# RWKV units of a hybrid decoder layer: which queue issues the value and gate loads of a unit's end

## The chip, the cores and the metric

The kernel runs on one core of a Trainium2 chip. The metric is the device time of one execution in microseconds (us), as the median of repeated runs. A core has a tensor engine (PE in the profile; its weight loads are PEld), a vector engine (DVE), a scalar engine (ACT), GpSimd (POOL) and a sync engine (SP). Each takes its instructions in order and waits on semaphores for the others. DMA transfers are issued by SP, ACT or POOL and carried out by 16 DMA engines.

## The reference

One layer on 1024 tokens of 1024 features, all in float32. One projection gives the columns of an attention group and of an RWKV-7 group; the two group outputs are concatenated and projected, and a feed-forward block follows.

```python
z = _rms_norm(x, norm_mix_pre) @ w_in
attn = _rms_norm(_dilated_attention(q, k, v), attn_out_gain)
rw = _rwkv7(r_r, k_r, v_r, xw, xa, xg, ...)
x = x + _rms_norm(concat([attn, rw]) @ w_out, norm_mix_post)
x = x + _rms_norm(square(relu(_rms_norm(x, norm_ffn_pre) @ w_ffn_up)) @ w_ffn_down, norm_ffn_post)
```

The change is in the RWKV-7 group. Its state S of 64 x 64 for each of 8 heads runs over the tokens, and the end of a unit is the second part of this:

```python
S_t = S_{t-1} diag(w_t) - (S_{t-1} kk_t)(kk_t*a_t)^T + v_t k_t^T ;  y_t = S_t r_t
yn = (y - mean) * rsqrt(var + GN_EPS) * gn_w + gn_b     # per head
out = (yn + sum(r*k*r_k) * v) * g                       # v: values, g: gate
```

## The kernel before, in words

The 1024 tokens are cut into 8 units of 128 tokens, and a unit into two chunks of 64 (c_ = 0, 1). For the RWKV group the kernel first works on pairs of heads (norms, pre_pair, subst, merge), which leave their results in DRAM, and then on the units. A unit n consists of

- `unit_ab`: loads AR and K, multiplies them on PE (p<-AR,K) and masks the products on DVE into T (L593). PE's p uses two PSUM banks in turn, so the next p waits until L593 has read the last.
- `unit_e`: E on PE from Zp and TR, evacuated by ACT (L618).
- `unit_c`, the recurrence, for each chunk: PE multiplies HV (O<-HV), ACT copies a half to VU (L654), PE multiplies VU (O<-VU), DVE adds into HV (L660) and scales it into the HV of the next chunk (L661); ACT copies the result to Y (L662), once L660 has been done. The next chunk's O<-HV needs L661.
- `unit_g`, the unit's end: loads bv (the values, from v_d) and gg (the gate, from g_d), works out the group norm of Y (L681 and the small steps after it), scales and shifts bv (L684, L685), and ends with L688 (Y + bv) and L689 (Y times gg). Y is then stored to r_d (L691).

bv and gg have one buffer each. The loads for unit n wait until L688 and L689 of unit n-1 have read theirs. Until the units begin, the same buffers serve other tiles of pre_pair.

Between these steps PE works off the projections z_aq, z_ak and z_avB of the attention group, in pieces of 0.7 us. z_aq and z_ak are split into a high part by ACT (evh, L721) and a low part by DVE (evl, L722), and the low part is stored to qk_d by POOL (L724).

What sets the order: `drive` runs through the jobs with a table of waiting times (`WAIT`) and writes out PE's and SP's instructions in that order, under `tc.manual_schedule`. The order of DVE, ACT and POOL is chosen by the scheduler, from when it expects an instruction's inputs; POOL's DMAs are among these. All engines then run in the order that was written.

The functions that the diff touches, with the line numbers of the profile (`G` is POOL, `nc.sync` is SP, `t5` takes a tile of 128 x 512 from the pool of the units):

## Time and profile before

| | |
|---|---|
| median of 3 runs | 1283.39 us (1283.11 to 1285.42) |
| the profiled execution | 1283.58 us |
| its span on the core | 1281.8 us |
| busy PE, DVE, ACT, POOL | 98%, 70%, 49%, 3% of the span |
| granted TensorE clock | 0.997 |
| the units (bv's loads) | 290.3 to 421.9 us of the span |

Times in rows of the timeline count from the start of the span: start, duration, engine, line, operation, out<-in with buffer numbers left out, form, and in brackets the idle time of the engine just before and what ended it. In rows of waits the figures are total us, number of times, longest. In rows of a tile the durations are min/median/max in ns. In rows of windows each stretch has the busy time of PE, PEld, DVE, ACT and POOL with their instruction counts, then the granted clock, the DMA share and GB/s. "To landing" is the time from the start of a DMA's issue until its data is there.

### The profile page before, as it was taken

How to read it: one execution, taken by the hardware profiler on the slowest of the kernel's cores; microseconds unless marked ns; L12 is line 12 of the kernel's file. 1: busy time of each engine (PE TensorE's matmuls, PEld its weight loads, DVE VectorE, ACT ScalarE, POOL GpSimd, SP SyncE). 2: the span in 40 equal slices, each digit the busy share in tenths (PEclk: the TensorE clock that was granted, in tenths of full speed). 3: DMA queues.
4: the chain of work that ended last, by engine and by line, in shares of the span. 5: the costliest groups of instructions: out<-in, count | busy, mean ns of one | idle time of the engine just before them, and what ended most of it. 6: DMA issues, size and time to landing. Idle time of an engine off the chain costs nothing.

```text
span 1281.8 us, 24136 instructions
## 1 busy us (share of the span) xinstructions
PE 1251.9 (98%) x9648; PEld 1043.8 (81%) x9648; DVE 897.4 (70%) x1643; ACT 621.7 (49%) x1048; POOL 43.2 (3%) x61
## 2 busy tenths in 40 slices
PE   6989999999999999999999999999999999999997
PEld 5778888898789788888887888888887888888886
DVE  7867779533777668767789877677666875446884
ACT  8653433234544378766565444344433544443442
POOL 0000000000000000000000000000000001000221
PEclk9999999999999999999999999999999999999999
DMA  6445767968875766234243653444467983555642
GB/s 246 146 181 160 207 164 196 278 188 261 252 240 151 271 238 208 70 104 145 104 151 138 204 159 139 154 163 146 151 231 249 363 322 109 183 193 197 197 160 103
DMA packets 165312, 241.10 MB, mean 188 GB/s; under 512 B 56304, under 2 KB 91376, under 8 KB 165200
## 3 DMA queue, kind: packets, MB, share of 16 engines
q1 hardware_dynamic: 154672, 213.86, 51.7%
q10 hardware_dynamic: 9088, 20.98, 5.0%
q0 software_dynamic: 1440, 4.72, 1.0%
q8 instruction: 76, 1.25, 0.4%
q14 instruction: 36, 0.29, 0.1%
HBM read 162.16 MB, written 77.09 MB: 187 GB/s over the span
## 4 chain that ended last, share of the span: by engine, by line
PE 79%; DVE 10%; DMA 5%; ACT 4%; issue 2%; SPq 0%; DVEq 0%; ACTq 0%
PE dX L50 12%; PE X L50 10%; PE pm L50 7%; PE dZ L50 7%; PE Z L50 5%; PE z_v L50 4%; PE dY L50 3%; PE z_ak L50 3%; PE z_r L50 3%; PE Y L50 3%; PE po L50 2%; PE z_aq L50 2%; PE pT L952 2%; PE pS L50 2%; PE z_avA L50 2%
## 5 line engine op out<-in xcount | busy, mean ns | idle before, releaser
L50 PE MATMUL dX<-wow,wou 128*128 128x512 f32 x768 | 175.5, 390 | 0.5 <-DVE wow L1271 0.5
L50 PEld LDWEIGHTS dX<-wow,wou 128*128 128x128 f32 x768 | 143.9, 188 | 31.5 <-DVE wow L1271 1.3
L50 PE MATMUL dZ<-wow,wou 128*128 128x512 f32 x384 | 87.4, 389 | 0.0
L50 PEld LDWEIGHTS dZ<-wow,wou 128*128 128x128 f32 x384 | 72.1, 188 | 15.0
L1271 DVE TENSOR_TENSOR wou<-ur,wou 128x1024 fp32r<-128x1024 f32 x56 | 71.2, 1273 | 6.1 <-ACT wou L1270 5.6
L1270 ACT ACTIVATE wou<-ur 128x1024 fp32r<-128x1024 f32 x56 | 58.5, 1048 | 21.1 <-DMA ur<-u_d 13.8
L1270 ACT ACTIVATE wow<-wd 128x1024 fp32r<-128x1024 f32 x32 | 33.8, 1060 | 68.4 <-PE dX L50 24.5
L1271 DVE TENSOR_TENSOR wow<-TK,wow 128x1024 fp32r<-128x1024 f32 x24 | 30.6, 1274 | 50.0 <-ACT wow L1270 50.0
L1271 DVE TENSOR_TENSOR wow<-wd,wow 128x1024 fp32r<-128x1024 f32 x32 | 39.5, 1237 | 26.9 <-ACT wow L1270 26.5
L1368 ACT ACTIVATE r<-u 128x512 f32<-128x512 f32 x48 | 30.1, 626 | 54.5 <-DVE u L1366 54.4
L1270 ACT ACTIVATE wow<-TK 128x1024 fp32r<-128x1024 f32 x24 | 25.4, 1059 | 62.9 <-PE dX L50 32.5
L942 ACT ACTIVATE S<-S,mn 128x1024 f32<-128x1024 f32 (+7 forms) x64 | 49.2, 769 | 7.6 <-DVE mn L940 6.2
L50 PE MATMUL pm<-WO,mxr 128*128 128x512 f32 x192 | 49.1, 400 | 0.0
L1576 POOL TENSOR_TENSOR E<-E,gpF 128x512 f32<-128x512 f32 x12 | 22.4, 1881 | 755.3 <-DMA xf<-x_d 595.1
L940 DVE CUSTOM_DVE_ANT_0 S<-pS,stripT 128x512 f32<-128x512 f32 (+3 forms) x64 | 37.4, 589 | 13.6 <-PE pS L50 13.1
L50 PE MATMUL pm<-WO,mxa 128*128 128x512 f32 x192 | 46.1, 395 | 0.1
L50 PE MATMUL Z<-HB,wo 128*128 128x512 f32 x192 | 46.1, 389 | 0.0
L952 PE MATMUL pT<-cst,S 128*128 128x128 f32 x288 | 43.6, 277 | 2.4 <-ACT PT L954 1.4
L50 PE MATMUL z_aq<-hT,wh_aq 128*128 128x512 f32 x128 | 44.3, 404 | 0.0
L50 PE MATMUL z_ak<-hT,wh_ak 128*128 128x512 f32 x128 | 44.0, 402 | 0.0
L50 PE MATMUL z_k<-hT,wh_k 128*128 128x512 f32 x128 | 43.8, 400 | 0.0
L50 PE MATMUL dY<-wow,wou 128*128 128x512 f32 x192 | 43.7, 389 | 0.0
(399 smaller groups left out, 3097.1 us busy)
## 6 DMA issues: line engine op xcount, KB each, us to landing
ur<-u_d SPq DMA_DIRECT2D x56, 512.0 KB, 4.2
u_d<-S SPq DMA_DIRECT2D x64, 256.0 KB, 2.4
wd<-in_wdown_dram SPq DMA_DIRECT2D x32, 512.0 KB, 4.5
u_d<-u SPq DMA_DIRECT2D x48, 256.0 KB, 2.5
TK<-in_wdown_dram SPq DMA_DIRECT2D x24, 512.0 KB, 6.6
wr_upa<-in_wup_dram SPq DMA_DIRECT2D x16, 512.0 KB, 3.6
wr_upb<-in_wup_dram SPq DMA_DIRECT2D x16, 512.0 KB, 4.1
x<-in_x_dram SPq DMA_DIRECT2D x8, 512.0 KB, 6.9
```

Of the source, the lines that this page charges most:

```text
L50: return PE.matmul(o, lhsT, rhs, start=start, stop=stop, skip_group_check=True)
L940: V.tensor_tensor_reduce(Sx[:, lo:hi], pS[:, :hi - lo], stripT[:, so:so + hi - lo], 1.0, 3e38 if k == 0 else mn[:, 0:1], OP.add, OP.min, a ...
L942: at["exp"] = A.activation(Sx[:, :w], Sx[:, :w], AF.Exp, scale=-1.0, bias=mn[:, nbk - 1:nbk], accum_out=at[p, "den"][:, i, h:h + 1])
L952: PE.transpose(pt[:, j], Sx[:, (4 * k + j) * P:(4 * k + j + 1) * P], ident)
L1270: A.activation(w[:, 0, 0:n], raw, AF.Copy)
L1271: low = E.tensor_tensor(w[:, 1, 0:n], raw, w[:, 0, 0:n].bitcast(F32), OP.subtract)
L1368: A.activation(r, src, AF.Relu)
L1576: G.tensor_tensor(e, e, gn[n], OP.mult)
```

## The change

The two loads of `unit_g` are issued by POOL instead of SP, for all 8 units:

```diff
             bv, gg = t5(f"bv{n}", "bv"), t5(f"gg{n}", "gg")
-            nc.sync.dma_start(bv, v_d[ts, :])
-            nc.sync.dma_start(gg, g_d[ts, :])
+            G.dma_start(bv, v_d[ts, :])
+            G.dma_start(gg, g_d[ts, :])
```

PE's instructions keep their order. SP's list loses 16 DMAs and keeps the order of the rest. The loads take places on POOL that the scheduler chooses, and with them it moves the instructions of DVE that use them. In the rows, the number behind a name is a buffer's: bv_3960 is unit 1's, bv_4193 unit 2's, bv_4287 unit 3's, bv_4892 unit 5's, and Y_3875 and Y_4540 are the Y of units 1 and 4.

On POOL, the loads of units 1 to 3 among the stores of evl (+ is new):

```order
 L724 DMA qk_d<-evl_aq_0_3853 128x512
+L673 DMA bv_3960<-v_d 128x512
+L674 DMA gg_3961<-g_d 128x512
 L724 DMA qk_d<-evl_aq_1_4072 128x512
+L673 DMA bv_4193<-v_d 128x512
+L674 DMA gg_4194<-g_d 128x512
+L673 DMA bv_4287<-v_d 128x512
+L674 DMA gg_4288<-g_d 128x512
 L724 DMA qk_d<-evl_ak_0_4331 128x512
```

Each load stands on POOL as an instruction that waits for its buffer to come free, and the stores behind it wait with it.

On DVE, where unit 1's end and the recurrence of unit 2 (HV) meet the masks of unit 4 (T):

```order
 L689 TENSOR_TENSOR Y_3875<-Y_3875,gg_3961 128x512
 L660 TENSOR_TENSOR HV_3838<-O_1_4155,HV_3838 64x512
+L684 TENSOR_TENSOR bv_4193<-bv_4193,BON 128x512
 L661 TENSOR_TENSOR HV_4057<-HV_3838,PcL 64x512
 L593 TENSOR_TENSOR T_4_4222<-p_4_0_4223,cst 128x512
 L593 TENSOR_TENSOR T_4_4222<-p_4_0_4224,cst 128x512
```

The first step on unit 2's values has moved ahead of L661 and of two masks; it stood some twelve instructions later.

On DVE, where unit 4's end and the recurrence of unit 5 meet:

```order
 L688 TENSOR_TENSOR Y_4540<-Y_4540,bv_4653 128x512
 L689 TENSOR_TENSOR Y_4540<-Y_4540,gg_4654 128x512
+L684 TENSOR_TENSOR bv_4892<-bv_4892,BON 128x512
+L685 TENSOR_TENSOR bv_4892<-bv_4892,gw_3502 128x512
 L660 TENSOR_TENSOR HV_4507<-O_1_4831,HV_4507 64x512
 L661 TENSOR_TENSOR HV_4771<-HV_4507,PcL 64x512
```

Both steps on unit 5's values now stand ahead of L660 and L661 of that unit. Units 1 and 4 have moved in the same way as unit 5, unit 3 as unit 2 (L684 between L660 and L661 of its first chunk). L684 of unit 0 has moved up into the substitution of the last pair (L503, L505), behind the second of its products. Units 6 and 7 keep their places on DVE.

## Prediction

> **What bounds the kernel now.** I read the page first (span, busy shares), then the windows of busy time, then the waits of the tensor engine, and last the tile bv and the timeline around each of its eight loads.

> ```profile
> span 1281.8 us, 24136 instructions
> PE 1251.9 (98%) x9648; PEld 1043.8 (81%) x9648; DVE 897.4 (70%) x1643; ACT 621.7 (49%) x1048; POOL 43.2 (3%) x61
> 290.00:436.00 146.00, 141.43 (x1958) 121.30 (x1953) 99.13 (x228) 69.26 (x115) 5.40 (x10) 1.00 0.73 227
> 342.00:346.00 4.00, 3.31 (x87) 3.10 (x88) 3.75 (x7) 1.46 (x3) 0.00 (x0) 1.00 1.03 362
> 388.00:392.00 4.00, 4.00 (x68) 3.51 (x66) 3.90 (x9) 2.89 (x5) 0.00 (x0) 1.00 0.02 4
> ```

> PE is busy 98% of the span and runs in an order written out by hand, so its idle time is all that the kernel can gain, and any new PE idle time is lost for good. The unit ends lie between 290 and 436 us: PE works 141.43 of 146.00 us there, so 4.6 us is the most that the change can win. The last two figures of a row are the DMA share and GB/s: the DMA engines are full at 342 to 346 us and empty at 388 to 392.

> The loads that move, and what PE waits for in this stretch (total, times, longest):

> ```profile
> L673 SPq DMA_DIRECT2D bv<-v_d x8: 314/423/458, 290.3 to 421.9; - x8
> L684 DVE TENSOR_TENSOR bv<-bv,BON x8: 683/692/694, 295.2 to 424.5; 128x512 f32<-128x512 f32 x8
> L685 DVE TENSOR_TENSOR bv<-bv,gw x8: 691/692/694, 295.9 to 425.2; 128x512 f32<-128x512 f32 x8
>   DMA bv<-v_d: 8.3, 5
> DMA to landing us min/median/max: 2.6/4.3/7.7
> PE O L50 <- ACT VU L654: 1.9, 3, 0.7
> PE p L50 <- DVE T L593: 0.6, 1, 0.6
> PEld O L50 <- DMA VU<-vc_d: 0.4, 1, 0.4
> ```

> DVE stands still 8.3 us for bv, five times. PE waits for none of these loads and hardly for any load (0.4 us); it waits for DVE and ACT, in the recurrence O, HV, VU and in the masks T. So the question is not how long SP takes to issue, but which DVE work stands behind L684 while its load is under way.

> **The change part by part.** *SP loses 16 issues.* At 0.42 us each that is 6.8 us of a queue that PE waits for by 0.4 us at most. I take 0; the gain is 0 to 0.4 us.

> *POOL gains 16 issues*, at the price of its other DMAs:

> ```profile
> L724 POOL DMA_DIRECT2D qk_d<-evl_aq x8: 539/540/710, 230.4 to 442.4; - x8
> DMA to landing us min/median/max: 2.8/5.1/8.2
> ```

> 16 x 0.54 is 8.6 us on an engine that is busy 5.4 of these 146 us: 0. Queued behind the loads are the stores of evl. A load waits for its slot (bv is free after L688 of the unit before, gg after L689), and by the DVE order each evl behind it is computed after that, so a store loses at most two issues, 1.1 us, and its reader is the attention part much later: 0. What counts is the landing time of a 256 KB load from POOL, which the trace does not show. The nearest rows are POOL's stores of that size (2.8 to 8.2, median 5.1) and the same loads from SP (2.6 to 7.7). I take 5.1, and SP's own landing in units 4 and 5, where the engines are less loaded.

> *DVE's order moves.* In units 1 to 5 L684 now stands earlier, with the recurrence behind it. Unit 2, the row of PE last and SP's old issue ahead of it:

> ```profile
> 343.54 0.69 DVE L688 TENSOR_TENSOR Y<-Y,bv 128x512 f32<-128x512 f32 x1
> 345.04 0.68 DVE L660 TENSOR_TENSOR HV<-O,HV 64x512 f32<-64x512 f32 x1
> 345.76 0.68 DVE L661 TENSOR_TENSOR HV<-HV,PcL 64x512 f32<-64x512 f32 x1
> 346.37 0.68 DVE L593 TENSOR_TENSOR T<-p,cst 128x512 f32<-128x512 f32 x1
> 353.11 0.69 DVE L684 TENSOR_TENSOR bv<-bv,BON 128x512 f32<-128x512 f32 x1 [2.38 <-DMA bv<-v_d]
> 345.36 0.42 SPq L673 DMA_DIRECT2D bv<-v_d  x1
> 347.10 0.49 PE L50 MATMUL p<-AR,K 64*128 64x128 f32 x2 [0.59 <-DVE T L593]
> ```

> POOL can issue bv when L688 of unit 1 ends: 344.2 as before, or up to 1.4 earlier, since L684 and L685 of unit 1 leave the stretch ahead; half of it gives 343.5. Landing 348.6. L684 then starts 3.6 us after L660; L661 and L593 follow 0.6 and 0.7 us apart, so L593 starts at 349.9 instead of 346.37. PE's p matmul already waits for it, so PE loses all of it: **+3.5**. In the kernel before, L684 came after this L593 and its wait hit nobody.

> Unit 5, with SP's landing time of this load, and the ACT steps that follow L660:

> ```profile
> 391.52 0.69 DVE L688 TENSOR_TENSOR Y<-Y,bv 128x512 f32<-128x512 f32 x1
> 394.21 0.68 DVE L660 TENSOR_TENSOR HV<-O,HV 64x512 f32<-64x512 f32 x1 [1.27 <-PE O L50]
> bv<-v_d SPq DMA_DIRECT2D x1, 256.0 KB, 4.6
> 394.93 0.59 ACT L662 ACTIVATE Y<-O 64x512 f32<-64x512 f32 x1 [0.61 <-DVE HV L660]
> 397.86 0.58 ACT L654 ACTIVATE VU<-O 64x512 f32<-64x512 f32 x1
> ```

> L688 ends at 391.5 (392.2 less 0.7 as above). Landing 4.6 later, 396.1; L684 and L685 now both stand ahead of L660: 397.5 instead of 394.21. ACT's L662 waits for L660, and from there ACT runs without a gap to VU, which PE takes next: **+3.3**.

> Units 1 and 4 have the same order (each with SP's landing of its load):

> ```profile
> 324.76 0.69 DVE L688 TENSOR_TENSOR Y<-Y,bv 128x512 f32<-128x512 f32 x1
> 331.79 0.68 DVE L660 TENSOR_TENSOR HV<-O,HV 64x512 f32<-64x512 f32 x1 [4.31 <-PE O L50]
> bv<-v_d SPq DMA_DIRECT2D x1, 256.0 KB, 7.5
> 374.60 0.67 DVE L688 TENSOR_TENSOR Y<-Y,bv 128x512 f32<-128x512 f32 x1
> 380.62 0.68 DVE L660 TENSOR_TENSOR HV<-O,HV 64x512 f32<-64x512 f32 x1 [2.94 <-issue]
> bv<-v_d SPq DMA_DIRECT2D x1, 256.0 KB, 4.0
> ```

> Unit 1: 325.5 + 5.1 + 1.4 = 332.0 against 331.79: **+0.2** (7.5 us, as SP's load took there, would give +2.6; 2.8 gives 0). Unit 4: 375.3 + 4.0 + 1.4 = 380.7 against 380.62: **+0.1** (5.1 would give +1.2).

> Unit 3 has L684 between L660 and L661; unit 0 has it in the substitution of pair 3:

> ```profile
> 356.70 0.69 DVE L688 TENSOR_TENSOR Y<-Y,bv 128x512 f32<-128x512 f32 x1
> 362.76 1.15 PE L50 MATMUL O<-HV,T 128*64 128x64 f32 x32
> 231.59 1.41 SPq L709 DMA_DIRECT2D v_d<-vt  x1
> 239.30 0.17 DVE L505 TENSOR_REDUCE Zt<-tmp 128x4 f32<-128x12 f32 x1
> 251.26 0.61 SPq L515 DMA_DIRECT2D z_d<-Zt  x1
> 264.70 1.29 DVE L593 TENSOR_TENSOR T<-p,cst 128x512 f32<-128x512 f32 x2 [16.08 <-PE p L50]
> ```

> Unit 3: unit 2's delay of 3.5 moves PE's matmul to 366.3; DVE uses up the 2.38 us that it stood at L684, so L688 moves by 1.1 and ends at 358.5; landing 363.6, L661 done at 364.9: 0. Unit 0: POOL's load waits for the store of v_d that SP issues at 231.6; with 5.1 to land for each, bv is there at 241.8, 2.4 us after the L505 behind which L684 now stands. That stall is hidden by DVE's 16.08 us of idleness ahead of 264.70 and by SP, which stores the finished Zt only at 251.26: 0. Units 6 and 7 keep their place on DVE: 0.

> The sum is 0.2 + 3.5 + 0.1 + 3.3 = 7.1 us. The profiled execution took 1283.58 us (span 1281.8 and 1.8 around it), 0.2 above the median of 1283.39; from the median the forecast is **1290.5 us**. The later stages run on a PE that is always behind, so nothing gives the time back.

> **The rivals.** *Short landings.* POOL's loads have a queue of their own and don't stand behind SP's AR, K and T loads; if all land in 2.8 us, POOL's shortest row, unit 1 and 4 cost 0, unit 2 gives 343.5 + 2.8 + 1.3 = 347.6 against 346.37, +1.2, and unit 5 gives 395.7 against 394.21, +1.5: 1286.1. Against it: 2.8 is one of 16 stores. [...]

> *Long landings.* The transfers share the DMA engines whoever issues them, and land as late as SP's in the same places (7.5, 7.7, 4.0, 4.6): +2.6, +6.1, +0.1, +3.3, 12.1 in all, 1295.5. For it speaks the full share at 342 to 346 us; against it that SP's loads also stood behind SP's own loads of AR, K and T. [...]

> *No change.* The stalls fall where PE has other work queued, as did the 8.3 us before: 1283.4. Against it: the p matmul's wait for T, which is there already.

> *Faster.* The loads leave some 1 us earlier and pass SP's queue, so DVE is never held and its two operations fill idle gaps; at most the 4.6 us of PE idleness go, 1278.8. This decides at a landing under 1.6 us in unit 2 (345.1 less 343.5) and 1.3 us in unit 5 (394.21 less 1.4 and 391.5); no row is that short, so it needs loads issued earlier than L688 allows.

> **How the numbers follow.** Forecast 0.56, long 0.14, short 0.14, no change 0.08, faster 0.08. A measurement tells 0.2%, 2.6 us, from no change. The short case ends at that edge and is shared out in halves: slower 0.56 + 0.14 + 0.07 = 0.77, the same 0.15, faster 0.08. The range goes from just under the short case to just over the long one, 1285.0 to 1296.0; it leaves out the last two cases and landings of 8 us throughout.

> **What would show it.** In the changed profile L684 of units 2 and 5 waits about 3 and 3.5 us for the load, right before an L661 and an L660; PE's p matmul waits about 4 us for T; ACT's L662 waits longer for L660; PE's busy time stays, its idle time from 290 to 443 us grows from 4.6 to about 11.7; bv's issue is on POOL 0.1 us after L688. I am wrong if the loads land in under 3 us, or if PE's delay in unit 2 turns the later waits of units 4 and 5 into slack.

## The result and the profile after

The kernel became slower: a median of 1296.02 us (1294.28 to 1296.92, 5 runs) against 1283.84 us (1283.11 to 1285.42, 5 runs) beside it, a ratio of 1.0089 (95% interval 1.0078 to 1.0100), 11 to 12 us. Run again on another chip the ratio was 1.0113 (1.0097 to 1.0129). The profiled execution shown here is the 1294.28 us one. Its page and what PE waits for at 210 to 480 us (total, times, longest):

```profile
span 1292.5 us, 24156 instructions
PE 1253.8 (97%) x9648; PEld 1046.2 (81%) x9648; DVE 897.3 (69%) x1643; ACT 621.0 (48%) x1048; POOL 52.0 (4%) x77
PE p L50 <- DVE T L593: 6.1, 1, 6.1
PE O L50 <- DVE HV L661: 2.8, 3, 1.7
PE O L50 <- ACT VU L654: 2.8, 4, 0.8
PE ptk L600 <- ACT TR L618: 1.4, 1, 1.4
PE z_avA L50 <- DVE evl_ak L722: 1.1, 1, 1.1
```

POOL has its 8.8 us of issues more and no engine waits for an instruction of POOL. PE's p matmul waits 6.1 us for T instead of 0.6 us, and its transposes ptk 1.4 us for ACT instead of 0.5 us. The timeline of unit 2 (POOL, DVE, then PE), and the tile bv:

```profile
342.30 0.54 POOL L673 DMA_DIRECT2D bv<-v_d  x1 [5.44 <-DVE Y L688]
344.00 0.68 DVE L660 TENSOR_TENSOR HV<-O,HV 64x512 f32<-64x512 f32 x1 [1.28 <-PE O L50]
349.66 0.69 DVE L684 TENSOR_TENSOR bv<-bv,BON 128x512 f32<-128x512 f32 x1 [4.97 <-DMA bv<-v_d]
350.27 0.68 DVE L661 TENSOR_TENSOR HV<-HV,PcL 64x512 f32<-64x512 f32 x1
350.87 1.27 DVE L593 TENSOR_TENSOR T<-p,cst 128x512 f32<-128x512 f32 x2
351.60 2.67 PE L50 MATMUL p<-AR,K 64*128 64x128 f32 x16 [6.13 <-DVE T L593]
  DMA bv<-v_d: 21.8, 7
DMA to landing us min/median/max: 2.9/4.4/7.3
```

The load is issued 0.3 us after L688 and lands 7.3 us later. Until then DVE stands at L684, and L661, the masks and PE stand behind it. All of DVE's waits for bv grew from 8.3 to 21.8 us. The windows of after show a second thing (the columns are those of the prediction; the granted clock is the third figure from the right):

```profile
330.00:350.00 20.00, 13.93 (x251) 11.74 (x245) 13.34 (x31) 10.04 (x17) 1.62 (x3) 1.00 0.83 251
350.00:352.00 2.00, 0.40 (x2) 0.40 (x2) 2.00 (x4) 0.00 (x0) 0.00 (x0) 0.58 0.06 23
352.00:360.00 8.00, 8.00 (x41) 6.26 (x40) 7.23 (x21) 2.33 (x4) 0.54 (x1) 0.50 0.20 66
360.00:362.00 2.00, 2.00 (x35) 1.63 (x35) 0.00 (x0) 0.43 (x1) 0.54 (x1) 0.86 0.50 108
sum 146.00, PE 132.35 PEld 113.36 DVE 91.41 ACT 67.21 POOL 11.37; mean PE 16.54 PEld 14.17 DVE 11.43 ACT 8.40 POOL 1.42
```

How far the profiled execution lags behind that of before can be followed along the same instructions. In the rows, the first of each pair is before, the second after:

```profile
238.31 0.55 POOL L724 DMA_DIRECT2D qk_d<-evl_aq  x1 [7.19 <-DVE Zt L505]
235.54 0.54 POOL L724 DMA_DIRECT2D qk_d<-evl_aq  x1 [1.04 <-DVE Zt L505]
284.36 0.54 POOL L724 DMA_DIRECT2D qk_d<-evl_aq  x1 [36.19 <-DVE evl_aq L722]
282.98 0.54 POOL L724 DMA_DIRECT2D qk_d<-evl_aq  x1 [33.94 <-DVE evl_aq L722]
337.44 0.54 POOL L724 DMA_DIRECT2D qk_d<-evl_aq  x1 [15.08 <-DVE rsm_gn L93]
336.31 0.55 POOL L724 DMA_DIRECT2D qk_d<-evl_aq  x1 [10.67 <-DVE rsm_gn L93]
366.46 0.54 POOL L724 DMA_DIRECT2D qk_d<-evl_ak  x1 [6.90 <-DVE evl_ak L722]
374.70 0.55 POOL L724 DMA_DIRECT2D qk_d<-evl_ak  x1 [9.39 <-DVE evl_ak L722]
389.74 0.68 DVE L660 TENSOR_TENSOR HV<-O,HV 64x512 f32<-64x512 f32 x1
404.75 0.69 DVE L684 TENSOR_TENSOR bv<-bv,BON 128x512 f32<-128x512 f32 x1 [3.78 <-DMA bv<-v_d]
406.08 0.68 DVE L660 TENSOR_TENSOR HV<-O,HV 64x512 f32<-64x512 f32 x1
```

The lag is -2.8 us ahead of the units. Most of that stems from 79 to 87 us: PE waited there 3.46 us for ACT (the step go, L364) in the execution of before and 1.71 us in that of after, and only in the one of before 3.4 us at a granted clock of 0.50 followed. Before (first three rows) and after:

```profile
82.48 0.96 PE L50 MATMUL g<-ghl,sgs 128*128 128x512 f32 x3 [3.46 <-ACT go L364]
84.00:86.00 2.00, 2.00 (x8) 1.71 (x7) 1.97 (x4) 1.99 (x3) 0.00 (x0) 0.50 0.32 124
86.00:88.00 2.00, 2.00 (x7) 1.59 (x7) 2.00 (x5) 0.60 (x1) 0.11 (x1) 0.69 0.00 0
80.73 0.96 PE L50 MATMUL g<-ghl,sgs 128*128 128x512 f32 x3 [1.71 <-ACT go L364]
82.00:90.00 8.00, 7.78 (x47) 6.17 (x48) 7.83 (x14) 5.82 (x9) 1.96 (x3) 1.00 0.35 135
```

The lag is then -1.4 us behind unit 0, -1.1 behind unit 1, +4.5 at unit 2's masks (350.87 against 346.37), +8.2 where the clock is whole again, +9.1 at unit 4's L660 (389.74 against 380.62) and +11.9 at unit 5's (406.08 against 394.21); at the end it is +10.7. So unit 0 cost 1.4, unit 1 0.3, unit 2 5.6, the slow clock 3.7, unit 4 0.9, unit 5 2.8, and 1.2 came back later.

### The profile page after: what moved, and what is told of

It reads as the page before. It is cut to its first block, busy times and chain, and to the rows that moved or that the text cites. A ratio compares the mean times of both kernels' runs of the same rounds, so it can differ in the third digit from the quotient of the medians.

```text
span 1292.5 us, 24156 instructions
## 1 busy us (share of the span) xinstructions
PE 1253.8 (97%) x9648; PEld 1046.2 (81%) x9648; DVE 897.3 (69%) x1643; ACT 621.0 (48%) x1048; POOL 52.0 (4%) x77
## 4 chain that ended last, share of the span: by engine, by line
PE 68%; issue 6%; DVE 4%; DMA 3%; ACT 2%; POOL 0%; SPq 0%; DVEq 0%; POOLq 0%; ACTq 0%
PE X L50 13%; PE dX L50 12%; PE pm L50 7%; PE dZ L50 7%; PE Z L50 7%; PE dY L50 3%; PE Y L50 3%; PE po L50 2%; PE pT L952 2%; PE z_aq L50 2%; PE pS L50 2%; PE z_ak L50 2%; PE z_avA L50 2%; PE z_avB L50 1%; PE O L50 1%
## 5 line engine op out<-in xcount | busy, mean ns | idle before, releaser
L50 PE MATMUL dX<-wow,wou 128*128 128x512 f32 x768 | 175.3, 389 | 0.6 <-DVE wow L1271 0.5
L50 PEld LDWEIGHTS dX<-wow,wou 128*128 128x128 f32 x768 | 144.0, 188 | 31.2 <-DVE wow L1271 1.0
L50 PE MATMUL dZ<-wow,wou 128*128 128x512 f32 x384 | 87.4, 389 | 0.0
L50 PEld LDWEIGHTS dZ<-wow,wou 128*128 128x128 f32 x384 | 72.1, 188 | 15.0
L1270 ACT ACTIVATE wou<-ur 128x1024 fp32r<-128x1024 f32 x56 | 58.5, 1048 | 14.4 <-DMA ur<-u_d 7.1
L50 PE MATMUL pm<-WO,mxr 128*128 128x512 f32 x192 | 49.2, 400 | 0.0
L940 DVE CUSTOM_DVE_ANT_0 S<-pS,stripT 128x512 f32<-128x512 f32 (+3 forms) x64 | 37.3, 589 | 13.7 <-PE pS L50 13.1
L50 PE MATMUL pm<-WO,mxa 128*128 128x512 f32 x192 | 46.0, 394 | 0.2 <-ACT mxa L1029 0.2
L50 PE MATMUL Z<-HB,wo 128*128 128x512 f32 x192 | 46.1, 389 | 0.0
L50 PE MATMUL z_ak<-hT,wh_ak 128*128 128x512 f32 x128 | 45.4, 414 | 0.0
L50 PE MATMUL z_aq<-hT,wh_aq 128*128 128x512 f32 x128 | 44.3, 404 | 0.0
L50 PE MATMUL dY<-wow,wou 128*128 128x512 f32 x192 | 43.7, 389 | 0.0
L50 PE MATMUL z_v<-hT,wh_v 128*128 128x512 f32 x128 | 43.1, 400 | 0.0
## 6 DMA issues: line engine op xcount, KB each, us to landing
u_d<-S SPq DMA_DIRECT2D x64, 256.0 KB, 2.4
u_d<-u SPq DMA_DIRECT2D x48, 256.0 KB, 2.3
```

The costliest lines, as they stand in the source:

```text
L50: return PE.matmul(o, lhsT, rhs, start=start, stop=stop, skip_group_check=True)
L940: V.tensor_tensor_reduce(Sx[:, lo:hi], pS[:, :hi - lo], stripT[:, so:so + hi - lo], 1.0, 3e38 if k == 0 else mn[:, 0:1], OP.add, OP.min, a ...
L1270: A.activation(w[:, 0, 0:n], raw, AF.Copy)
```

## The experiments

They ran in three groups, each on one chip, with the kernel before beside them (medians 1284.74, 1284.76 and 1285.54 us; four rows of the table each). A ratio is formed from all executions of both kernels and is not quite the quotient of the two medians; where a ratio is given in us below, it is of these medians. The theory, ORDER, is the prediction's: the time is lost because DVE meets L684 earlier and holds back L660, L661 and L593. The rival POOL is that issuing from POOL, its queue or its transfers cost the time themselves. CLOCK is what the windows above suggested: PE's long wait slows PE's clock.

| kernel | what differs | median us | ratio to before (95%) |
|---|---|---|---|
| e1_order_before | all on POOL, DVE order as before | 1284.03 | 1.0000 (0.9981 to 1.0018) |
| e7_sp_order_unit2 | all on SP, L684 early in unit 2 | 1291.12 | 1.0056 (1.0036 to 1.0077) |
| e2_order_unit2 | as changed, unit 2's order as before | 1291.18 | 1.0043 (1.0026 to 1.0060) |
| e3_order_units45 | as changed, units 4 and 5 as before | 1291.85 | 1.0055 (1.0037 to 1.0072) |
| r2_changed_again | the changed kernel | 1298.53 | 1.0113 (1.0097 to 1.0129) |
| e6_fill_stall | PE works in most of the wait | 1294.53 | 1.0078 (1.0060 to 1.0095) |
| e8_two_slots | two buffers for bv | 1298.05 | 1.0109 (1.0093 to 1.0125) |
| e9_two_slots_held | two buffers, L684 held back | 1282.76 | 0.9987 (0.9978 to 0.9997) |
| e4_gates_only | only gg on POOL | 1285.50 | 1.0002 (0.9989 to 1.0015) |
| e5_values_only | only bv on POOL | 1297.60 | 1.0103 (1.0088 to 1.0118) |
| e11_fill_all | PE works in all of the wait | 1291.34 | 1.0053 (1.0041 to 1.0066) |
| e10_sp_two_slots | e9 with loads on SP | 1285.34 | 1.0004 (0.9993 to 1.0015) |

### Who pays: the order or POOL

e1 keeps all loads on POOL and ties L684 and L685 to an instruction behind which they stood before (`R_` keeps the instructions by name: vr is L681, gn2 unit 2's second L93, HV3 L661 of unit 3's first chunk, T1 a mask of unit 1). e2 ties unit 2 alone, e3 units 4 and 5.

```diff
+            at = {0: ("T1", 0), 1: ("vr1", 0), 2: ("gn2", 1), 3: ("HV3", 0), 4: ("vr4", 0), 5: ("vr5", 0)}.get(n)
+            with (tc.issue_after(R_[at].ins) if at else contextlib.nullcontext()):
-            V.tensor_tensor(c8(bv), c8(bv), bc(R["BON"][:, n].rearrange("p q h -> p (q h)"), 64), OP.mult)
-            V.tensor_tensor(bv, bv, R["gwb"][1], OP.add)
+                V.tensor_tensor(c8(bv), c8(bv), bc(R["BON"][:, n].rearrange("p q h -> p (q h)"), 64), OP.mult)
+                V.tensor_tensor(bv, bv, R["gwb"][1], OP.add)
```

> All 16 loads stay on POOL; L684 and L685 are held where they stood on DVE in the kernel before (unit 0's L684 two places earlier). Theory ORDER (the time is lost because DVE stands at L684 ahead of L660, L661 and L593): the whole +12.2 us goes, 1283.5 to 1284.5 us; L684 may still wait for its load, but PE's 6.1 us wait for T and the slow clock after it are gone. Rival POOL (issue by POOL, its queue or its transfers cost the time themselves): 1295 to 1297 us, as in the changed kernel. A time between, say 1288, would mean that both have a share.

e1 takes 1284.03 us, ratio 1.0000. PE's wait for T and DVE's waits for bv in e1 (its lines stand 2 to 4 lower than in the kernel before: L595 is the mask):

```profile
PE p L50 <- DVE T L595: 0.6, 1, 0.6
  DMA bv<-v_d: 8.0, 4
```

Both are back at the values of before (0.6 and 8.3). POOL issues all 16 loads and that costs nothing that the interval shows: 0.18%, 2.3 us, at most. The counterpart, e7, leaves all loads on SP and moves unit 2's L684 ahead on DVE, and its load ahead of the store of unit 1's Y on SP. In its trace unit 3's L684 and L685 also stand some instructions later than in the kernel before:

```diff
+                    if n == 2 and c_ == 1:
+                        R["bv2"] = t5("bv2", "bv")
+                        nc.sync.dma_start(R["bv2"], v_d[n * P:(n + 1) * P, :])
+                        lead = R["lead"] = V.tensor_tensor(c8(R["bv2"]), c8(R["bv2"]), ..., OP.mult)
+                    with (tc.issue_after(lead.ins) if lead else contextlib.nullcontext()):
                         V.tensor_tensor(dst, HV[lo, c_], ..., OP.mult)
...
+                    with (tc.issue_after(R["lead"].ins) if n == 4 and c_ == 0 else contextlib.nullcontext()):
                         V.tensor_tensor(T1[:, h, c_], pp[h], mask..., OP.mult)
```

> All 16 loads on SP, as in the kernel before; only in unit 2 L684 is put ahead of L661 and of the two L593 of unit 4 on DVE (SP issues this one load ahead of the store of unit 1's Y instead of behind it). ORDER: DVE stands at L684 until SP's load has landed; with SP's own landing of 7.7 us there, from 344.2, the masks start at 353.3 instead of 346.4 and PE's p waits some 7 us more: 1291 by the stall alone, 1293.5 to 1294.5 with the slow clock after it (CLOCK). POOL: 1283.8, since no load is issued by POOL.

```profile
350.67 0.69 DVE L666 TENSOR_TENSOR bv<-bv,BON 128x512 f32<-128x512 f32 x1 [2.56 <-DMA bv<-v_d]
351.88 1.27 DVE L594 TENSOR_TENSOR T<-p,cst 128x512 f32<-128x512 f32 x2
352.61 2.67 PE L50 MATMUL p<-AR,K 64*128 64x128 f32 x16 [7.34 <-DVE T L594]
```

Without a single load on POOL, PE waits 7.34 us for T and the kernel is 0.56% (7.2 us) slower: ORDER holds, POOL falls. The median of 1291.12 us is 2 to 3 us under the 1293.5 to 1294.5 expected with CLOCK and equal to the 1291 expected without it. The interval, 4.6 to 9.9 us over the kernel before, holds both, so this time doesn't tell them apart. In the profiled execution the lag grows by 9.7 us between 337 and 375 us, and the clock is at 0.50 for 10.2 us. The two partial repairs share out the loss:

> As the changed kernel, but L684 and L685 of unit 2 alone are held where they stood before. ORDER with CLOCK (the 6.1 us stall of PE costs 5.6 us more than before, and the half-speed clock after it another 2.5): 8.1 us less than the changed kernel, 1287.9 us, and a granted clock of 1.00 from 350 to 362 us of the span. ORDER with a clock that drops for another reason: 5.6 less, 1290.4, the clock still 0.5 for some us. POOL: no gain, 1296.

> As the changed kernel, but L684 and L685 of units 4 and 5 alone are held where they stood before. ORDER: 0.9 (unit 4) and 2.8 (unit 5) less than the changed kernel, 1292.3 us, with the 6.1 us stall and the slow clock of unit 2 still there. If those later shifts were only echoes of unit 2: no gain, 1296. POOL: 1296.

With unit 2 repaired (e2) 0.43% is left, with units 4 and 5 repaired (e3) 0.55%: 5.5 and 7.1 us. Together they are 12.6 us; units 0 and 1, which are in both, count twice in it with 1.7 us, so the two parts come to about the whole. e2 came out 3 us above its expectation of 1287.9. The kernel before is 0.9 us slower on this chip, and the interval of e2, 3.3 to 7.7 us over it, holds the 4.1 us that the expectation amounts to. Its executions spread from 1286.4 us at a mean granted clock of 0.999 to 1294.5 us at 0.995, and those of the kernel before beside it as widely, from 1280.8 us at 0.998 to 1290.2 us at 0.995: a slow clock comes in some executions of either kernel. In e2's profiled execution the clock is 1.00 from 348 to 380 us, in that of e3 it is 0.50 for 10 us again, so the slow clock goes with unit 2's wait.

### Which of the two loads

> Only gg is loaded by POOL; bv stays on SP. DVE and ACT keep the order of the kernel before in every row. ORDER: 1283 to 1285, equal to the kernel before within 2 us, since nothing is moved ahead of L660, L661 or L593. POOL: eight of the sixteen issues and half of the bytes, so about half of the loss, 1290.

> Only bv is loaded by POOL; gg stays on SP. DVE and ACT have the order of the changed kernel in every row. ORDER: the whole loss, 1294 to 1299, less at most 1 to 2 us if bv lands sooner without a gg of its own queue behind it. POOL: half of the loss, 1290.

With only the gates on POOL, DVE's order is that of before in every row, and so is the time (1.0002). With only the values on POOL, DVE's order is that of the changed kernel, and so is the loss (1.0103 against 1.0089 and 1.0113). The number of issues plays no part, nor does a gg right behind bv.

### The clock

e6 lets PE repeat unit 4's transposes into the same banks while it waits; e11 does the same with 10 instead of 7. The small steps of unit 2's norm and ACT's copies are held so that DVE and ACT keep their order.

```diff
-                    for cq in range(8):
-                        for h in range(2):
-                            PE.transpose(pt[h][:, cq], ...)
+                    for _ in range(7 if n == 4 else 1):
+                        for cq in range(8):
+                            for h in range(2):
+                                PE.transpose(pt[h][:, cq], ...)
```

> The changed kernel itself once more, beside the next three on the same chip, as their measure: about 1.009 of the kernel before, with PE's wait of some 6 us for T near 345 us and about 10 us of granted clock 0.50 behind it.

> As the changed kernel, but the transposes ptk of unit 4 (16 of them, 0.6 us) are done seven times instead of once, into the same banks with the same values, so that PE works some 3.6 us of the 6.1 us in which it waits for T; DVE, ACT, POOL and SP keep their order but for one neighbouring pair on DVE. Theory CLOCK (the granted clock falls because PE stands still for 6 us): the p matmul starts as late as before, the clock stays at 1.00 and the time is 2.5 us (0.2%) under the changed kernel. Rival (the clock falls for another reason, or the slow clock costs nothing because later waits take it up): the same time as the changed kernel, within 0.5 us, or with a slow clock all the same.

> As e6_fill_stall, with ptk of unit 4 done ten times instead of seven, some 5.3 us of work in a wait of 5 to 6 us. CLOCK: no slow period is left behind this wait (in e6 1.2 us of wait were left, and 3.5 us of half speed followed), and the time is another 1 to 1.5 us lower than in e6, about 1293; by the waits alone, without the clock, it could not be lower than the changed kernel. Rival (the slow clock belongs to the place, not to the wait): half speed after 350 us as before.

Rows of windows of e6 (first), then of e11 (last two):

```profile
354.00:358.00 4.00, 4.00 (x19) 2.96 (x15) 3.66 (x14) 1.70 (x3) 0.00 (x0) 0.57 0.21 68
350.00:352.00 2.00, 2.00 (x70) 2.00 (x68) 0.00 (x0) 0.00 (x0) 0.00 (x0) 1.00 1.06 225
354.00:362.00 8.00, 7.83 (x119) 6.45 (x118) 7.56 (x22) 3.63 (x7) 0.00 (x0) 1.00 0.27 85
```

In e6 PE still waited 1.44 us for T and the slow time behind it shrank to 3.4 us (4 us at a mean of 0.57); another of 6.8 us came behind a wait of 2.64 us in unit 5. In e11 PE had work but for 1.19 us and the clock stayed at 1.00, although DVE stood at L684 for 4.86 us as before. e11 does 144 transposes more than the changed kernel and is faster: 1.0053 against 1.0103 of e5, which has the DVE order of the changed kernel, beside it on the same chip. The mean granted clock was 0.997 to 0.999 in all five executions of e11 and 0.992 to 0.993 in all four of e5. CLOCK holds. How the loss divides is less sure. e11 is 6.8 us (5.3 to 8.5) over the kernel before and e5 13.2 (11.3 to 15.2), which leaves the clock some 6 us, an estimate, 3 to 10 by the ends of the intervals; in the profile shown above, where only one slow time falls into the units, it was 3.7 us. In e11's own profiled execution, the slowest of its five, the span was still 10.2 us longer than in that of before (1292.0 against 1281.8 us), without a slow time in the units, so the waits themselves differ from execution to execution.

### Would an earlier load help?

e8 gives bv two buffers in turn (a buffer that only the pairs had used serves odd units). e9 does so with L684 and L685 held back as in e1, in units 6 and 7 too; e10 is e9 with the loads on SP.

```diff
-            bv, gg = t5(f"bv{n}", "bv"), t5(f"gg{n}", "gg")
+            bv = R["p"].tile([P, 576], F32, name=f"bv{n}", tag="P")[:, 0:512] if n % 2 else t5(f"bv{n}", "bv")
+            gg = t5(f"gg{n}", "gg")
```

> As the changed kernel, but bv has two buffers in turn (odd units use one that only the pairs used before). The scheduler then issues each load a unit ahead and also does L684 and L685 a unit ahead, at the same places on DVE as in the changed kernel, where the load has just been issued (its buffer is set free by the L688 of two units before). ORDER: the DVE stall in front of L661 and L593 is there for the next unit's values instead: 1293 to 1297 us. Rival LATENCY (it is enough to load earlier, the places on DVE don't matter): 1283 to 1285.

> Two buffers for bv and the loads on POOL, with L684 and L685 held behind L681 of their own unit (unit 2 behind its second L93, unit 3 behind L661 of its first chunk, unit 0 behind a mask of unit 1), so that each load has a whole unit to land. ORDER: DVE's 8 us of waits for bv are gone and PE's waits are those of the kernel before: 1283 to 1285, equal to the kernel before within 1.5 us. FASTER (those waits cost PE something after all): up to 4 us less than the kernel before, 1280.

> The two buffers and the held order of e9, with all loads on SP again. If the 2 us that e9 stood under the kernel before come from loading a unit ahead: the same time as e9, 1282 to 1284. If they come from POOL issuing (SP's queue relieved): back to the kernel before, 1284.5. The two lie within what one comparison tells apart, so the waits in the trace decide: DVE waiting for bv at all, PE waiting for T and HV.

In the first three rows, of e8, the load of unit 3's values goes out, the step on them (L685 there) waits for it during unit 2, and PE waits for T. The last row has the landings in e9, where the tile's rows name no wait for the load any more:

```profile
345.94 0.54 POOL L674 DMA_DIRECT2D bv<-v_d  x1 [5.44 <-DVE Y L689]
352.67 0.69 DVE L685 TENSOR_TENSOR bv<-bv,BON 128x512 f32<-128x512 f32 x1 [4.34 <-DMA bv<-v_d]
PE p L50 <- DVE T L593: 5.5, 1, 5.5
DMA to landing us min/median/max: 3.5/5.0/7.6
```

A second buffer alone changes nothing (1.0109): the scheduler moves the steps on the values a unit ahead together with their load, and DVE stands in front of the same L661, now for the next unit's values. With the steps held back, DVE never waits for bv, and e9 is the fastest of all: 1282.76 us. Its interval, 0.9978 to 0.9997, lies just under the kernel before, by 0.4 to 2.8 us. e10 on SP stands at 1.0004 with 4.7 us of DVE waits left. The intervals of e9 and e10 overlap and they ran on different chips, so whether POOL's issue has a share in e9's gain stays open. Of PE's waits of before, those for VU (1.9 us) and T (0.6) are still there in e9; that for HV fell from 1.3 to 0.6 us.

## Why the prediction was right, and where it was not

The forecast was 1290.5 us, +7.1; the medians measured are 12.2 us apart. 1296.02 us lies 0.02 us over the top of the stated range, 1296.0. The kernel before was 0.45 us slower here than the 1283.39 us that the forecast started from; by the ratio, 1.0089 times 1283.39 us is 1294.8, inside the range. The direction and the cause were right. That the time came near the rival of long landings (1295.5) is partly coincidence: that rival put +2.6, +6.1, +0.1 and +3.3 on units 1, 2, 4 and 5, measured were 0.3, 5.6, 0.9 and 2.8, and the rest came from two terms that neither sum had, unit 0 and the slow clock.

- *POOL's and SP's issues at 0*: right (e1 1.0000, e4 1.0002).
- *DVE's order as the cause*: right, and shown from both sides: order undone with loads on POOL (e1, 1.0000), order done with loads on SP (e7, 1.0056).
- *Unit 2, +3.5*: the mechanism right, the size not. The term rests on a landing of 5.1 us; it was 7.3, and the masks came 5.6 us late. 5.1 was no bad choice for a typical landing (medians of 4.2 to 5.2 over the kernels whose bv comes from POOL), but this load was slower than that in every one of them that has a single buffer for bv, 5.7 to 8.0 us. The DMA engines are full there (share 0.97 and 0.98 from 340 to 348 us), and SP's own load had taken 7.7. For units 4 and 5 the prediction took SP's landing at the same place, 4.0 and 4.6, and came close: 4.6 and 4.2.
- *Unit 5, +3.3, and unit 1, +0.2*: 2.8 and 0.3. *Unit 4, +0.1*: 0.9; its load took 0.5 us longer than the 4.0 assumed, and the loss shows as ptk's wait for ACT. *Unit 3 at 0*: right, its L684 at 365.53 us doesn't wait.
- *Unit 0 at 0*: wrong. I looked at the substitution's L505 behind L684 and at its slack, not at everything behind L684. Between the two stood an evl_ak of the projections:

```profile
240.44 0.69 DVE L684 TENSOR_TENSOR bv<-bv,BON 128x512 f32<-128x512 f32 x1 [3.92 <-DMA bv<-v_d]
241.05 0.69 DVE L722 SCALAR_TENSOR_TENSOR evl_ak<-z_ak,evh_ak 128x512 fp32r<-128x512 f32 x1
248.26 0.50 PE L50 MATMUL z_avA<-wh_avA,hT 128*128 128x256 f32 x2 [1.12 <-DVE evl_ak L722]
```

  PE's z_avA waits for a later evl_ak (1.12 us), and the lag grew by 1.4 us there.
- *The slow clock*: missing from the sum altogether. At 3.7 us in the profile and some 6 us (3 to 10) by e11 it is the largest error. "PE's busy time stays" failed with it: 1251.9 became 1253.8. The trace of before had such a price in it: 3.46 us of wait on PE before 82.48 us, and behind it 3.4 us at a granted clock of 0.50. A forecast that puts a 4 us wait on PE should have carried one, and the prediction didn't.
- *What would show it*: all of it came, most of it larger, but for PE's busy time. L684 waits 4.97 and 3.78 (about 3 and 3.5 forecast), p waits 6.1 (about 4), the issue comes 0.3 us behind L688 (0.1), PE's idle time from 290 to 443 us is 13.7 us (11.7), and ACT's L662 of unit 5 waits 3.20 us for L660 where it had waited 0.61.

With 7.3 in place of 5.1, 1.4 for unit 0 and 3.7 for the clock the same sum gives 14.4 us, against 14.7 by the lags before the 1.2 us that came back, which the prediction had ruled out ("nothing gives the time back"). The medians, 12.2 and 13.8 us apart on two chips, fit that.

## What to carry to other kernels

Moving a load to another queue can change the order in which the engines consume it: compare each engine's order first, and for each consumer that moved ahead of other work ask when its load lands and everything that now stands behind it. A consumer tied to where its value is needed made the load's issuer, and nearly its latency, irrelevant (e1, 1.0000 with landings of 3.4 to 7.9 us); another buffer alone did not, as the consumer moved ahead with the load (e8, 1.0109). A landing is best read at its own place and not as a median: unit 2's load was the slow one with either issuer (7.3 us from POOL, 7.7 from SP, against medians of 4.4 and 4.3). And a wait of 5.0 to 7.3 us on PE cost more than its length here, because the granted clock was 0.50 for 7 to 14 us around its end.

## What the runs showed of the hardware

The slow times of these profiles lasted 3.4, 6.8, 10.2 or 13.7 us. From the rows of windows below (after the changed kernel's three above): e1, the changed kernel again, and e5.

```profile
368.00:370.00 2.00, 1.25 (x26) 1.15 (x24) 1.66 (x11) 0.00 (x0) 0.00 (x0) 0.63 1.04 307
370.00:372.00 2.00, 2.00 (x18) 1.78 (x14) 1.25 (x2) 0.59 (x1) 0.00 (x0) 0.51 1.07 239
352.00:354.00 2.00, 0.77 (x4) 0.68 (x6) 2.00 (x4) 0.20 (x1) 0.00 (x0) 0.81 0.12 35
354.00:360.00 6.00, 6.00 (x36) 4.99 (x36) 5.49 (x19) 2.14 (x4) 0.00 (x0) 0.50 0.28 82
360.00:362.00 2.00, 2.00 (x35) 1.51 (x35) 1.36 (x2) 0.00 (x0) 0.84 (x2) 0.98 0.00 0
346.00:350.00 4.00, 1.08 (x28) 0.94 (x24) 0.29 (x1) 2.31 (x4) 0.00 (x0) 0.91 1.01 245
350.00:352.00 2.00, 0.00 (x0) 0.00 (x0) 1.00 (x2) 0.00 (x0) 0.00 (x0) 0.50 0.39 145
352.00:362.00 10.00, 9.06 (x49) 7.08 (x51) 8.56 (x23) 2.33 (x4) 0.55 (x1) 0.50 0.18 53
362.00:364.00 2.00, 2.00 (x33) 1.84 (x30) 0.00 (x0) 0.59 (x1) 0.00 (x0) 0.76 0.79 236
```

What is missing to 1.00, times the stretch, over 0.5, gives the time at a granted clock of 0.50: 3.4 us in e1 (behind PE gaps of 2.2 us in all), 6.8 in the second run of the changed kernel (gap 5.0), 10.2 in the first (6.1), 13.7 in e5 (5.9). The clock fell 4.9 us after PE stopped in the changed kernel and 2.2 us after it in e5, and it came back 9.0 us after PE had gone on in the one, 10.0 in the other. Behind a wait of 1.44 us in e6 it was 3.4 us, behind the 1.71 us at 79 us in the changed kernel none.

So in these runs the length of PE's wait alone did not tell whether the clock fell. Two rows of e7, then two of e8:

```profile
76.86:80.27 3.41, 1.96 (x9) 1.29 (x7) 1.51 (x4) 1.34 (x5) 0.00 (x0) 1.00 0.43 157
80.27:83.69 3.42, 2.21 (x14) 1.94 (x15) 0.77 (x2) 2.40 (x7) 0.00 (x0) 1.00 0.60 230
993.85:997.27 3.42, 1.79 (x7) 1.18 (x8) 2.34 (x3) 3.42 (x4) 0.00 (x0) 1.00 0.67 240
997.27:1000.68 3.41, 3.41 (x10) 2.67 (x9) 3.41 (x5) 0.47 (x1) 0.00 (x0) 0.50 1.00 359
```

In the two rows of e7 PE is busy for 1.96 and 2.21 us, idle for 2.66 us of 6.83, and the clock is 1.00 in both. In the first row of e8 PE is busy for 1.79 us, idle for 1.63 us of 3.42, and the next 3.41 us, with PE busy throughout, are at 0.50. What decides between the two, and what brings the clock back, these runs have not shown.
